# A batched trace of matrix products on one Trainium2 core: loads issued in strict order, smaller last loads with five rows for TensorE, and a first tile cut into five loads

**Chip, cores, metric.** One core of one Trainium2 chip. The metric is the device time of one execution in microseconds (us); medians of several executions are given.

## The reference

```python
def setup_inputs():
    B, N = 8, 2176
    return {"a": np.random.randn(B, N, N).astype(np.float32),
            "b": np.random.randn(B, N, N).astype(np.float32)}

def reference(a, b):
    prod = np.matmul(a, b)
    traces = np.diagonal(prod, axis1=1, axis2=2).sum(axis=-1)
    return traces.astype(np.float32)
```

The trace of A·B is the sum of the elementwise product of A transposed and B. So there is no matrix product to make: both inputs (303 MB in f32) are read once, A is transposed, and products are summed.

## The kernel before

A row in this text is a block of 128 matrix rows by 2176 columns; a batch has 17 of them (0 to 16). Only where the first tile is cut up, and in shares per DMA engine, a row is one matrix row (8704 bytes in f32). GpSimd issues the loads, which turn f32 to bf16 on the way. TensorE transposes A, ScalarE and VectorE copy the result out of PSUM, and VectorE multiplies it with B and sums, one row an instruction. In the last batch some rows are given to TensorE instead (a chain of 128x128 products into one PSUM tile, whose diagonal is the wanted sum): seven whole rows (every odd one up to 13) and parts of 14, 15 and 16. The last row comes in three pieces.

```python
    stage = ctx.enter_context(tc.tile_pool(name="stage", bufs=3))
    single = ctx.enter_context(tc.tile_pool(name="single", bufs=2))
    ...
    def load(src, start, m, count):
        if m == 1:
            t = single.tile([P, 1, N], bf16, tag="single")
        else:
            t = stage.tile([P, DOUBLE * ROWS, N], bf16, tag="stage")
        ...
        issued = nc.gpsimd.dma_start(out=part, in_=rows)
    ...
    def load_first(src, start):          # one row of A, in f32, by SyncE
        ...
        nc.sync.dma_start(out=plain, in_=src[start:start + P, :])
        nc.scalar.copy(out=t[:, 0, :half], in_=plain[:, :half])
        nc.vector.tensor_copy(out=t[:, 0, half:], in_=plain[:, half:])
    ...
        for start, m, count in joined(b_groups):      # joined: two groups of 4 in one load
            if last and start == N - P:
                b_t = stage.tile([P, DOUBLE * ROWS, N], bf16, tag="stage")
                row = b_t[:, 0, :]
                for g0, g1 in LAST_PIECES:            # [(0, 2), (2, 3), (3, 5)]
                    lo, hi = g0 * WIDE, min(g1 * WIDE, N)
                    nc.gpsimd.dma_start(out=row[:, lo:hi], in_=b[bi, start:start + P, lo:hi])
                ...
            for start, m, b_t in groups:
                for s in range(m):
                    if last and (m == 1 or s % 2 == 1):
                        half = 2 if m == 1 else 0
                        multiply_on_pe(at, row, v0 + s, half, len(a_groups))
                        if half:
                            on_dve(wide_at(at, v0 + s, 0, half), wide(row, 0, half))
                    else:
                        on_dve(wide_at(at, v0 + s, 0, n_wide), wide(row, 0, n_wide))
```

The framework decides from these when a load may be issued: the tile pools hand out buffers, and a load waits until the last reader of its buffer is done.

## Time and profile before

| | before |
|---|---|
| time, us (median; 711.01 to 711.58) | 711.17 |
| span of the profiled run, us | 709.4 |
| 16 DMA engines | 90% or more busy in 39 of 40 slices |
| VectorE / TensorE / ScalarE busy | 58% / 29% / 28% |
| rows 12-13 landed; row 14; row 15; third piece of row 16 | 699.75; 694.59; 702.42; 705.07 |
| pieces of row 16 issued | 691.92 |

The landings are worked out from the trace's completion signals: a load sends 16, one from each DMA engine, and is taken as landed with the last. The lines that carry the reading are in the prediction below. The view of the three pieces' tile says how early they were issued: the columns of its first line are least, median and longest duration in ns, then first and last start in us.

```profile
L247 POOL DMA_DIRECT2D b_t<-in_b_dram x3: 528/536/548, 691.9 to 693.0; - x3
DMA to landing us min/median/max: 11.7/11.8/12.1
```

Some 12 us pass from issue to landing, since the queue ahead of them is full. Such a wait costs nothing: a load that waits behind others keeps the engines fed.

### The profile page before, as it was taken

What the parts mean: (1) busy time and instruction counts of PE and PEld (TensorE: products, weight loads), DVE (VectorE), ACT (ScalarE), POOL (GpSimd) and SP (SyncE); (2) the same over time, 40 slices, a digit from 0 to 9 for tenths busy, and PEclk for the clock granted to TensorE, in tenths of its full rate; (3) what the DMA queues carried; (4) which work ended last, traced back from release to release, by engine and by line L of the source; (5) the groups of instructions that cost most, each with busy time, mean ns of one, the idle gap of its engine ahead of it and who ended that gap; (6) DMA issues with size and microseconds to landing.
All of it is one profiled execution on the core that took longest, in us unless ns stands there. A gap on an engine that the chain in (4) does not pass through costs nothing.

```text
span 709.4 us, 3709 instructions
## 1 busy us (share of the span) xinstructions
PE 206.3 (29%) x1406; PEld 193.0 (27%) x1406; DVE 411.4 (58%) x449; ACT 196.8 (28%) x210; POOL 34.6 (5%) x60
## 2 busy tenths in 40 slices
PE   1542005420065100542006510065100560005655
PEld 0542005410065100541005510065000550005655
DVE  0223996139952399514994259932599335993356
ACT  2443005430064200633006420065200651006610
POOL 1000000000010000100000000000000000000000
PEclk9977557765577655766557665577655775557776
DMA  9999999999999999999999999999999999999996
GB/s 220 220 220 219 206 219 220 219 217 209 219 220 218 217 212 216 220 219 215 212 218 220 218 213 215 215 222 217 215 214 213 225 217 212 215 217 222 219 207 138
DMA packets 11620, 152.32 MB, mean 215 GB/s; under 512 B 850, under 2 KB 1106, under 8 KB 3282
## 3 DMA queue, kind: packets, MB, share of 16 engines
q0 software_dynamic: 11456, 150.97, 100.1%
q1 hardware_dynamic: 146, 1.11, 0.4%
q8 instruction: 11, 0.18, 0.1%
q14 instruction: 7, 0.06, 0.0%
HBM read 303.04 MB, written 0.00 MB: 427 GB/s over the span
## 4 chain that ended last, share of the span: by engine, by line
DMA 56%; DVE 34%; issue 7%; PE 2%; another core or an unknown queue 2%; POOL 0%; DVEq 0%; POOLq 0%
DMA t<-in_b_dram 43%; DVE scratch L122 33%; DMA t<-in_a_dram 13%; PE ps L155 1%; DVE acc L122 0%; DVEq L122 0%; PE ps L176 0%; POOL identity masks.py:199 0%; DVE at L110 0%; POOL identity masks.py:197 0%; PE total L298 0%; DVE result L302 0%; DVE late L122 0%; POOLq L74 0%
## 5 line engine op out<-in xcount | busy, mean ns | idle before, releaser
L122 DVE CUSTOM_DVE_ANT_1 scratch<-at,t 128x2048 bf16<-128x2048 bf16 (+1 forms) x156 | 310.6, 1991 | 74.9 <-DMA t<-in_b_dram 67.7
L112 ACT COPY at<-ps 128x1024 bf16<-128x1024 bf16 x208 | 194.4, 1044 | 474.9 <-PE ps L155 474.5
L155 PE MATMUL ps<-identity,t 128*128 128x128 f32 x1071 | 177.9, 334 | 482.5 <-DVE sums L275 262.7
L155 PEld LDWEIGHTS ps<-identity,t 128*128 128x128 f32 x1071 | 166.2, 213 | 490.8 <-DVE sums L275 311.2
L110 DVE COPY at<-ps 128x1024 bf16<-128x1024 bf16 (+2 forms) x104 | 93.5, 902 | 214.4 <-PE ps L155 196.9
L74 POOL DMA_DIRECT2D t<-in_a_dram x23 | 15.3, 663 | 354.3 <-PE ps L176 156.5
L74 POOL DMA_DIRECT2D t<-in_b_dram x26 | 16.8, 645 | 288.3 <-PE ps L176 147.5
L283 PEld LDWEIGHTS <-at 128*128 128x128 bf16 x153 | 17.1, 122 | 13.3 <-issue 12.7
L283 PE MATMUL trace_ps<-t,at 128*128 128x128 bf16 x144 | 16.7, 293 | 12.3 <-DMA t<-in_b_dram 12.3
L176 PE MATMUL ps<-identity,t 128*128 128x128 bf16 x170 | 16.4, 219 | 4.9 <-DVE at L110 4.8
L176 PEld LDWEIGHTS <-t 128*128 128x128 bf16 x170 | 13.0, 100 | 8.3 <-issue 8.0
L122 DVE DVE_READ_ACCUMULATOR2_ANT acc<- 128x1 f32 x163 | 13.3, 81 | 0.0
L86 DVE CAST t<-words 128x1088 bf16<-128x1088 f32 x1 | 0.7, 726 | 4.8 <-DMA words<-in_a_dram 4.8
L247 POOL DMA_DIRECT2D b_t<-in_b_dram x3 | 1.6, 537 | 16.0 <-DVE acc L122 16.0
L122 DVE CUSTOM_DVE_ANT_0 scratch<-at,t 128x128 bf16<-128x128 bf16 x7 | 2.0, 291 | 0.2
L85 ACT CAST t<-words 128x1088 bf16<-128x1088 f32 x1 | 1.1, 1099 | 3.7 <-DMA words<-in_a_dram 3.7
L122 DVE CUSTOM_DVE_ANT_1 scratch<-at,b_t 128x256 bf16<-128x256 bf16 (+1 forms) x3 | 1.5, 510 | 0.1
L275 DVE TENSOR_REDUCE sums<-acc 128x1 f32<-128x22 f32 (+1 forms) x8 | 1.4, 174 | 0.3
L85 ACT ACT_TABLE_LOAD x1 | 1.3, 1283 | 0.7 <-PEq L321 0.7
L283 PE MATMUL trace_ps<-b_t,at 128*128 128x128 bf16 x9 | 1.3, 284 | 0.4 <-DMA b_t<-in_b_dram 0.4
L298 PE MATMUL total<-late,ones 128*1 128x1 f32 x8 | 0.8, 164 | 0.8 <-DVE late L122 0.8
L298 PEld LDWEIGHTS total<-late,ones 128*1 128x1 f32 x8 | 0.3, 80 | 1.2 <-DVE late L122 1.2
(14 smaller groups left out, 2.7 us busy)
## 6 DMA issues: line engine op xcount, KB each, us to landing
t<-in_a_dram POOLq DMA_DIRECT2D x16, 4352.0 KB, 46.7
t<-in_b_dram POOLq DMA_DIRECT2D x15, 4352.0 KB, 51.5
t<-in_b_dram POOLq DMA_DIRECT2D x9, 544.0 KB, 54.5
t<-in_a_dram POOLq DMA_DIRECT2D x7, 544.0 KB, 53.0
t<-in_b_dram POOLq DMA_DIRECT2D x1, 2176.0 KB, 42.9
words<-in_a_dram SPq DMA_DIRECT2D x1, 1088.0 KB, 4.9
t<-in_b_dram POOLq DMA_DIRECT2D x1, 1088.0 KB, 25.7
b_t<-in_b_dram POOLq DMA_DIRECT2D x1, 256.0 KB, 11.7
```

Source lines behind the costliest of these rows:

```text
L74: issued = nc.gpsimd.dma_start(out=part, in_=rows)
L85: nc.scalar.copy(out=t[:, 0, :half], in_=plain[:, :half])
L86: nc.vector.tensor_copy(out=t[:, 0, half:], in_=plain[:, half:])
L110: last_copy = nc.vector.tensor_copy(out=dst, in_=src)
L112: nc.scalar.copy(out=dst, in_=src)
L122: nc.vector.tensor_tensor_reduce(out=out, in0=x, in1=y, scale=1.0, scalar=0.0, op0=MUL, op1=ADD, accum_out=acc,)
L155: nc.tensor.transpose(ps[:, n * m + r, :], words[:, r, c0:c0 + step * (P - 1) + 1:step], tiles[f32],)
L176: last_transpose = nc.tensor.transpose(ps16[:, n, r, :], a_t[:, r, c0:c0 + P], tiles[bf16],)
L247: nc.gpsimd.dma_start(out=row[:, lo:hi], in_=b[bi, start:start + P, lo:hi])
L275: nc.vector.reduce_sum(out=tiles["sums"][:, bi:bi + 1], in_=acc[:, :cols], axis=mybir.AxisListType.X)
L283: nc.tensor.matmul(trace_ps, x, y, start=(n == 0), stop=(n == len(pe_work) - 1),)
L298: nc.tensor.matmul(total[:, BATCH - 1:BATCH], tiles["ones"], part, start=(n == 0), stop=(n == len(parts) - 1),)
```

## The change

Its intent: feed the DMA queue in program order, shorten what is left to do when the last bytes come (smaller last loads; TensorE gets rows 11, 12, 13 and 15 whole and most of 16, VectorE the others), and share the first tile differently over the 16 DMA engines. The diff, without its imports and empty lists (cuts marked with ...):

```diff
+    PE_ROWS = (11, 12, 13, 15)
+    FIRST_SPLIT = [(32, P, 1), (0, 32, 4), (1, 32, 4), (2, 32, 4), (3, 32, 4)]
...
+    def in_order():
+        return tc.issue_after(loaded[-1].ins) if loaded else nullcontext()
...
-        issued = nc.gpsimd.dma_start(out=part, in_=rows)
+        with in_order():
+            issued = nc.gpsimd.dma_start(out=part, in_=rows)
+        loaded.append(issued)
...
-        nc.sync.dma_start(out=plain, in_=src[start:start + P, :])
+        for lo, hi, step in FIRST_SPLIT:
+            nc.sync.dma_start(
+                out=plain[lo:hi:step, :], in_=src[start + lo:start + hi:step, :]
+            )
...
-        for start, m, count in joined(b_groups):
+        for start, m, count in ([(*g, 1) for g in b_groups] if last else joined(b_groups)):
...                                        (the pieces of the last row: in order, too)
-                    if last and (m == 1 or s % 2 == 1):
-                        half = 2 if m == 1 else 0
-                        multiply_on_pe(at, row, v0 + s, half, len(a_groups))
-                        if half:
-                            on_dve(wide_at(at, v0 + s, 0, half), wide(row, 0, half))
+                    if last and v0 + s in PE_ROWS:
+                        multiply_on_pe(at, row, v0 + s, 0, len(a_groups))
```

More of the change, by code (lines that the diff above doesn't have):

```diff
@@ L1 @@
 import math
-from contextlib import ExitStack
+from contextlib import ExitStack, nullcontext
 import concourse.bass as bass
@@ L64, in joined @@
         return loads
+    loaded = []
+    def in_order():
+        return tc.issue_after(loaded[-1].ins) if loaded else nullcontext()
     def load(src, start, m, count):
@@ L246 @@
                     lo, hi = g0 * WIDE, min(g1 * WIDE, N)
-                    nc.gpsimd.dma_start(out=row[:, lo:hi], in_=b[bi, start:start + P, lo:hi])
+                    with in_order():
+                        loaded.append(nc.gpsimd.dma_start(
+                            out=row[:, lo:hi], in_=b[bi, start:start + P, lo:hi]
+                        ))
                 multiply_on_pe(at, row, v0, 0, 1)
```

## The prediction

> **What bounds the kernel now.** I first read the forty slices and the queue table of the page, to see whether any compute engine matters at all.
>
> ```profile
> DVE  0223996139952399514994259932599335993356
> DMA  9999999999999999999999999999999999999996
> GB/s 220 220 220 219 206 219 220 219 217 209 219 220 218 217 212 216 220 219 215 212 218 220 218 213 215 215 222 217 215 214 213 225 217 212 215 217 222 219 207 138
> q0 software_dynamic: 11456, 150.97, 100.1%
> ```
>
> The 16 DMA engines are at 90% or more in all slices but the last, at a steady 205 to 225 GB/s; VectorE has long empty stretches in every batch. Loads from GpSimd take 100.1% of 16 engines' span for 150.97 MB (bf16 as landed). So the time is a head (until the engines run), the bytes at a fixed rate, and a tail (after the last bytes). The change leaves the bytes alone, so it can move only head, tail, and holes in the DMA queue. That is decided in the last 50 us, for which I read the timeline.
>
> ```profile
> 0.74 0.40 SPq L84 DMA_DIRECT2D words<-in_a_dram  x1
> 5.70 1.10 ACT L85 CAST t<-words 128x1088 bf16<-128x1088 f32 x1 [3.68 <-DMA words<-in_a_dram]
> ...
> 661.27 5.73 PE L155 MATMUL ps<-identity,t 128*128 128x128 f32 x28 [12.47 <-DMA t<-in_a_dram]
> 675.10 0.36 DVE L110 COPY at<-ps 128x384 bf16<-128x384 bf16 x1 [0.88 <-PE ps L176]
> 681.80 8.21 PE L283 MATMUL trace_ps<-t,at 128*128 128x128 bf16 x72 [6.74 <-DMA t<-in_b_dram]
> 691.92 1.59 POOL L247 DMA_DIRECT2D b_t<-in_b_dram  x3 [16.03 <-DVE acc L122]
> 692.07 4.22 PE L283 MATMUL trace_ps<-t,at 128*128 128x128 bf16 x36 [2.05 <-DMA t<-in_b_dram]
> 699.91 2.29 DVE L122 CUSTOM_DVE_ANT_1 scratch<-at,t 128x2048 bf16<-128x2048 bf16 x1 [3.09 <-DMA t<-in_b_dram]
> 702.24 1.23 DVE L122 CUSTOM_DVE_ANT_1 scratch<-at,t 128x1024 bf16<-128x1024 bf16 x1
> 703.51 1.22 DVE L122 CUSTOM_DVE_ANT_1 scratch<-at,t 128x1024 bf16<-128x1024 bf16 x1
> 704.86 0.68 DVE L122 CUSTOM_DVE_ANT_1 scratch<-at,b_t 128x512 bf16<-128x512 bf16 x1
> 705.11 0.45 PE L283 MATMUL trace_ps<-b_t,at 128*128 128x128 bf16 x3 [0.41 <-DMA b_t<-in_b_dram]
> 706.05 0.42 DVE L122 CUSTOM_DVE_ANT_1 scratch<-at,b_t 128x256 bf16<-128x256 bf16 x1
> 706.67 0.29 DVE L122 CUSTOM_DVE_ANT_0 scratch<-identity,trace_ps 128x128 bf16<-128x128 f32 x1 [0.18 <-DVE late L122]
> 707.42 0.32 SPq L303 DMA_DIRECT2D out_dram<-result  x1
> ```
>
> Three things stand here. The last bytes (the third piece of the last row) reach TensorE at 705.11. VectorE is unbroken from 699.91 to 706.96, so it, not the landing, sets the end by about a microsecond. And the three pieces of the last row were issued at 691.92, some 12 us before they landed: the queue never ran dry.
>
> One more fact comes from the trace's completion signals, 16 for each load, one a DMA engine. At the first whole load the 16 come within 0.45 us. The spread grows whenever a fetch on the two instruction queues (18 packets, 16 KB and 8 KB) falls on an engine: 1.58 at 68 us, 2.64 at the end. The third piece's signals run from 702.42 to 705.07, at lags of 0 to 0.57 us (six engines), 1.20 to 1.54 (seven) and 2.27 to 2.64 (three). The mean is 1.18, so perfect balance would land it 1.46 us earlier.
>
> **What the Trainium skill says.** "DMA: Bandwidth & Descriptors", section "Why a DMA increments its semaphore by 16 and not by 1": a DMA is spread over the largest count up to 16 that divides its slowest dimensions, on a SyncE queue over the lowest-numbered engines. A load of 96 rows then takes 6 rows on each of 16; a load of 8 rows takes engines 0 to 7. The trace agrees for 128 rows (16 signals; the split of 8 rows isn't in it). Its section "Latency and other measured facts" puts the first byte of a GpSimd DMA at about 1 us; no load here met an empty queue, so the trace can't confirm it. "Runtime: NRT & Kernel Launch", "Instruction fetch mechanics": instructions are refilled in blocks of 16 KiB by each sequencer's own DMA queue; the trace agrees with its 11 packets of 16384 bytes on the instruction queue, some 0.9 to 1.0 us each.
>
> **The change part by part.** *Strict order.* The built programs show that from the third batch on the single A tile was issued before the second A double; now it comes after. Neither position drains the queue (the last A double was issued at 614.16 and landed at 661, so over 20 us of work lay ahead of it). Worth to DMA: 0. The last double lands one row earlier: a row of 128x2176 f32 is 1.11 MB, at 434 GB/s read (twice the 217 GB/s that land as bf16 from 10 to 661 us) 2.57 us. Its transposes start at 658.5 and VectorE is free for B at 672.6 instead of 675.5.
>
> *Groups of 4, 4, 4, 2, 1, 1.* Landings, counted back at 2.57 us a row from row 15's 702.4 with the bytes unmoved: rows 0-3 at 671.4, 4-7 at 681.7, 8-11 at 692.0, 12-13 at 697.2, 14 at 699.75, 15 at 702.4.
>
> *Rows 11, 12, 13, 15 and most of 16 for TensorE.* VectorE now has 12 full rows (0 to 10 and 14) against 7 full and 2 halves; at some 2.37 us a row, 28.4 us against 19. It isn't on the path until the end: rows 0-3 from 672.6 to 682.1, 4-7 to 691.6, 8-10 from 692.1 to 699.2, row 14 from 699.85 to 702.2. It then waits for the pieces, where before it was busy until 704.8. With landings unmoved that takes 0.94 us off the end: the last small product starts at 705.15 in place of 706.05 (and the sum trims the rest). TensorE loses 64 matmuls, none of them last.
>
> *Where the gain goes.* In the built program the pieces' tile is put into the buffer of rows 12-13, and their issue waits for the last matmul of these two rows (before: the buffer of the first B load, free at 691.9). Those are 34 matmuls at 0.117 us (36 took 4.22), so 4.0 us after 697.2: 701.2. With 0.53 us for an issue and near 0.9 to the first byte (estimate, from the skill's 1 us) pieces flow from 702.6. The engines finish row 15 between 699.7 and 702.4, so all stand empty, 1.7 us on the mean. The pieces' 24 packets on each engine take 8 x (0.173 + 0.098 + 0.116) = 3.1 us, the signal 0.3: the last landing is 706.0, 0.9 later than before. That eats the 0.94.
>
> From the last landing to the end: 0.7 us to the start of the trace product, and 709.4 - 706.67 = 2.73 after it, 3.43 in all. 706.0 + 3.43 = 709.4: the old span.
>
> *First tile split.* 96 rows over 16 engines (6 each) and four loads of 8 rows over eight engines (4 more on each) make 10 rows on eight and 6 on the others, against 8. A row's packet takes 0.328 us, so 0.66 us are shifted, and stay shifted since the queue never drains. If the eight that get less are those that fetches hold up, every last signal moves by -0.66: rows 12-13 land at 696.5 and all that hangs on them comes 0.66 earlier. If it is the wrong side, +0.66. The split only makes sense if its author saw the former, but nothing in this trace names the engine of a packet: I give it two in three. Its own cost at the head (five issues of 0.4 us, the cast perhaps some us later) is hidden, since the next load that needs that buffer has until 46 us.
>
> Sum: 0 (bytes) - 0.94 (VectorE tail) + 0.9 (late pieces) and -0.66 or +0.66. Measured times lie 1.75 above the profiled span: 710.5 if the split helps, 711.2 if it does nothing, 711.9 if it hurts.
>
> **Rivals.** *The pieces come in time* (the 34 matmuls go faster, or first bytes need less than I think): then -0.94 - 0.66 = 709.6. Against it: 36 matmuls took 4.22 us in both late groups. *The bubble is worse* (first byte after 2 us, or TensorE reaches these rows late): 711.5 to 712. For it: GpSimd's issue is not measured on an empty queue here. *VectorE becomes the bound*: 12 rows are 28.4 us and it has from 672.6 to 702.4, with a slack of some 1.4 us; if copies of A end 3 us later than I count, row 14 ends at 703.5 and still before the last piece. Worth at most +0.5. *Strict order opens a hole* when an earlier load's buffer is late: would show as a slice under 200 GB/s and cost several us; buffers come free 20 us ahead, so one in thirty. *All is hidden*: a head and tail of some 10 us in 711 can't give 2% (14 us) either way.
>
> **Range and chances.** The three cases of the split, weighed, give 710.8. The uncertain terms are first byte and bubble (0.5 us each way), split (0.66), execution noise (0.2). Eight in ten: 709.6 to 712.0. A 2% change needs 14.2 us: no mechanism above has it.
>
> **What would show it.** The pieces' issue near 701 with TensorE's product as releaser (not 692); VectorE idle before its 128x512 product; the last landing at 705.3 to 706.6; a spread of the last signals near 2 us if the split is right, near 3.3 if wrong; 64 matmuls fewer. Wrong would be: an issue near 692, a middle slice that sags, or an end over 3.5 us after the last landing.

## The result, and the profile after

713.32 us (713.26 to 713.57) against 711.17: 2.15 us slower, outside the range of 709.6 to 712.0. The ratio is 1.003, with a 95% interval of 1.0013 to 1.0047. (Ratios here are the mean time of one kernel's fast runs over that of the other's of the same rounds, so not quite the ratio of the medians.)

The slices and the queue table of the changed kernel:

```profile
GB/s 211 219 218 218 209 224 212 218 219 213 221 218 214 215 219 219 218 213 217 213 219 218 218 214 218 215 217 216 218 216 218 212 218 216 218 218 211 219 214 116
q0 software_dynamic: 11472, 150.97, 99.8%
q1 hardware_dynamic: 178, 1.11, 0.6%
```

The middle is unmoved (217 GB/s from 10 to 700 us in both kernels); the slices that differ by more than the scatter are the first (211, was 220) and the last (116, was 138). So strict order made no hole, and the loss lies in head and tail. The chain of waits that ended last, in its final stretch (start, duration, what):

```profile
683.73 14.87 DMA t<-in_b_dram
698.64 4.08 PE trace_ps L299 x34
703.00 1.04 POOL b_t L264 x2
704.04 4.28 DMA b_t<-in_b_dram
708.37 0.50 PE trace_ps L299 x3
```

Before, this stretch was landings and VectorE alone. Now it goes from a landing (rows 12-13) to 34 products on TensorE, to GpSimd's issue, to the pieces' landing: the step foretold under "where the gain goes". The timeline has the same events with the releaser of each:

```profile
0.74 3.22 SPq L98 DMA_DIRECT2D words<-in_a_dram  x5
16.48 0.73 DVE L102 CAST t<-words 128x1088 bf16<-128x1088 f32 x1 [15.61 <-DMA words<-in_a_dram]
...
673.53 0.36 DVE L126 COPY at<-ps 128x384 bf16<-128x384 bf16 x1 [0.87 <-PE ps L192]
698.64 4.17 PE L299 MATMUL trace_ps<-t,at 128*128 128x128 bf16 x35 [2.75 <-DMA t<-in_b_dram]
703.00 1.60 POOL L264 DMA_DIRECT2D b_t<-in_b_dram  x3 [17.68 <-PE trace_ps L299]
703.89 2.12 PE L299 MATMUL trace_ps<-t,at 128*128 128x128 bf16 x17 [1.08 <-DMA t<-in_b_dram]
706.73 0.69 DVE L138 CUSTOM_DVE_ANT_1 scratch<-at,b_t 128x512 bf16<-128x512 bf16 x1 [2.86 <-DMA b_t<-in_b_dram]
708.45 0.43 DVE L138 CUSTOM_DVE_ANT_1 scratch<-at,b_t 128x256 bf16<-128x256 bf16 x1 [0.54 <-DMA b_t<-in_b_dram]
709.07 0.29 DVE L138 CUSTOM_DVE_ANT_0 scratch<-identity,trace_ps 128x128 bf16<-128x128 f32 x1 [0.18 <-PE total L314]
```

Set these beside the lines of before: VectorE now stands idle for 2.86 us until the first piece comes, where it was working without a break. GpSimd was held 17.68 us, and its releaser is TensorE. Row 15, which was the last thing in the queue, has landed by 703.85, but the pieces' first bytes come at 704.24: all 16 engines stood empty. The view of the pieces' tile confirms it from its own side, with a landing only some 4 us after the issue:

```profile
L264 POOL DMA_DIRECT2D b_t<-in_b_dram x3: 533/548/558, 703.0 to 704.0; - x3
DMA to landing us min/median/max: 3.7/3.8/4.3
```

A short time from issue to landing is bad news here: nothing was queued ahead.

The completion signals show the second loss. This table is worked out from the trace of each kernel; "mean" is the mean of the 16 signals of row 15's load, "excess" the last minus the mean.

| kernel | row 15 first | mean | last | excess | third piece |
|---|---|---|---|---|---|
| before | 699.71 | 700.89 | 702.42 | 1.53 | 705.07 |
| changed | 699.86 | 701.65 | 703.85 | 2.20 | 708.33 |
| e1, no split | 699.95 | 701.18 | 702.62 | 1.44 | 706.95 |
| e2, own buffer | 699.76 | 701.52 | 703.74 | 2.22 | 706.41 |
| e3, both | 700.04 | 701.26 | 702.84 | 1.58 | 705.55 |
| e4, split alone | 699.92 | 701.61 | 703.66 | 2.05 | 706.36 |
| e5, e3 with an even split | 700.65 | 701.99 | 703.57 | 1.58 | 706.31 |
| e7, e3 with a strided split | 700.40 | 701.66 | 702.97 | 1.31 | 705.62 |
| e8, e3 with double skew | 699.39 | 701.64 | 704.53 | 2.89 | 707.24 |
| e9, strict order alone | 700.02 | 701.26 | 702.73 | 1.47 | 705.28 |
| e11, e3 again | 699.99 | 701.02 | 702.53 | 1.51 | 705.25 |
| e12, e9 again | 699.87 | 701.06 | 702.82 | 1.76 | 705.15 |

The last two rows show the noise of one profile: the same kernel's mean moved by 0.2 us, its excess by up to 0.3.

### The profile page after: what moved, and what is told of

The parts are those of the page before. It is cut to its first block, busy times and chain, and to the rows that moved or that the text cites. A ratio compares the mean times of both kernels' runs of the same rounds, so it can differ in the third digit from the quotient of the medians.

```text
span 711.8 us, 3598 instructions
## 1 busy us (share of the span) xinstructions
PE 195.4 (27%) x1342; PEld 181.4 (25%) x1342; DVE 420.5 (59%) x455; ACT 196.5 (28%) x210; POOL 35.0 (5%) x61
## 4 chain that ended last, share of the span: by engine, by line
DMA 57%; DVE 35%; issue 5%; PE 2%; SPq 0%; ACT 0%; POOL 0%; another core or an unknown queue 0%; DVEq 0%; POOLq 0%; ACTq 0%
DMA t<-in_b_dram 48%; DVE scratch L138 34%; DMA t<-in_a_dram 6%; DMA words<-in_a_dram 2%; PE ps L171 1%; PE trace_ps L299 1%; DMA b_t<-in_b_dram 1%; DVE at L126 1%; DVE acc L138 0%; SPq L98 0%; ACT L101 0%; ACT t L101 0%; POOL b_t L264 0%; PE ps L192 0%
## 5 line engine op out<-in xcount | busy, mean ns | idle before, releaser
L138 DVE CUSTOM_DVE_ANT_1 scratch<-at,t 128x2048 bf16<-128x2048 bf16 (+1 forms) x159 | 319.6, 2010 | 76.4 <-DMA t<-in_b_dram 68.9
L171 PE MATMUL ps<-identity,t 128*128 128x128 f32 x1071 | 173.9, 328 | 484.3 <-DMA t<-in_a_dram 301.3
L171 PEld LDWEIGHTS ps<-identity,t 128*128 128x128 f32 x1071 | 162.1, 213 | 493.2 <-DVE sums L291 376.9
L299 PEld LDWEIGHTS <-at 128*128 128x128 bf16 x89 | 9.8, 124 | 25.4 <-issue 24.7
L299 PE MATMUL trace_ps<-t,at 128*128 128x128 bf16 x80 | 9.7, 291 | 22.8 <-DMA t<-in_b_dram 22.3
```

The lines of the kernel that those rows point to most:

```text
L138: nc.vector.tensor_tensor_reduce(out=out, in0=x, in1=y, scale=1.0, scalar=0.0, op0=MUL, op1=ADD, accum_out=acc,)
L171: nc.tensor.transpose(ps[:, n * m + r, :], words[:, r, c0:c0 + step * (P - 1) + 1:step], tiles[f32],)
L299: nc.tensor.matmul(trace_ps, x, y, start=(n == 0), stop=(n == len(pe_work) - 1),)
```

## The experiments

Each run was taken in the same rounds and on the same chip as the kernel before, whose median there is given in brackets. The runs e1 to e4 shared their rounds; so did e5 to e9 (no e6), and e10 to e12. The changed kernel was measured in another call (before: 711.17), so differences inside a group are the safer ones.

Theory A: the change has three effects. Strict order gains; the split loses; and the pieces' wait for TensorE's rows loses. Rivals: B, the split is harmless; C, order or smaller groups make holes in the queue; D, VectorE with 12 rows is the bound.

**e1: no split.**

```diff
-    FIRST_SPLIT = [(32, P, 1), (0, 32, 4), (1, 32, 4), (2, 32, 4), (3, 32, 4)]
+    FIRST_SPLIT = [(0, P, 1)]
```

> The changed kernel with its first tile loaded by one transfer of 128 rows again. Theory A (the split costs 1.4 us: rows 12-13 landed at 698.60 in place of 697.17, and it moves every last signal; the pieces' wait is a separate loss): rows 12-13 land near 697.2, the pieces' issue comes at 701.6 and not 703.0, the third piece lands near 706.9, spread of the 16 signals of row 15's load 2.6 us (4.0 in the changed kernel), time 712.0 +- 0.3. Rival B (the split is harmless, the whole loss is the pieces' wait for TensorE): 713.3. Rival C (strict order or the smaller B groups make holes in the queue): 713.3 too, with middle slices lower than before.

Measured: 712.16 (before, same rounds: 711.42), rows 12-13 landed at 697.37, the issue came at 701.77, the third piece at 706.95. As theory A had it; B and C are out. The split costs 1.2 us by the medians (713.32 - 712.16), 1.4 if each is taken against the kernel before in its own rounds.

**e2: a buffer of its own for the last row.**

```diff
+    tail = ctx.enter_context(tc.tile_pool(name="tail", bufs=1))
-                b_t = stage.tile([P, DOUBLE * ROWS, N], bf16, tag="stage")
+                b_t = tail.tile([P, 1, N], bf16, tag="tail")
```

> The changed kernel with the last row's tile in a buffer of its own, so that its three pieces wait for no other buffer; the split stays. Theory A: pieces issued near 685, right behind row 15; no empty queue; they land 2.65 us behind row 15's 703.9, at 706.5 in place of 708.3; span 709.9, time 711.7 +- 0.3. Rival B (the pieces' wait is the whole loss): landing at 705.1 and time near 710.2. Rival D (VectorE's 12 rows are the bound, the pieces only seem late): time stays at 713.

Measured: 711.67 (before 711.42). From its timeline, the issue of the pieces and VectorE's last products on them:

```profile
685.15 1.62 POOL L265 DMA_DIRECT2D b_t<-in_b_dram  x3
705.00 0.69 DVE L139 CUSTOM_DVE_ANT_1 scratch<-at,b_t 128x512 bf16<-128x512 bf16 x1 [1.25 <-DMA b_t<-in_b_dram]
706.54 0.43 DVE L139 CUSTOM_DVE_ANT_1 scratch<-at,b_t 128x256 bf16<-128x256 bf16 x1 [0.36 <-DMA b_t<-in_b_dram]
```

The last product starts at 706.54, not 708.45. The pieces' wait costs 1.65 us by the medians (713.32 - 711.67), 1.9 by the landings (708.33 against 706.41) and 1.8 inside one group of rounds (e1 - e3, 712.16 - 710.38). D is out: VectorE works the same 12 rows and waits for landings. The rows are not the matter but which buffer the pieces are put in.

**e3: both edits.**

> Both undone: first tile in one transfer, last row's tile in its own buffer; strict order, groups of 4, 4, 4, 2, 1, 1 and the five TensorE rows stay. Theory A: last landing 705.1 as in the kernel before, then 3.45 us to the end, where the kernel before needs 4.33: span 708.5, time 710.3 +- 0.3, 0.9 faster than before. Rival C (order or groups cost something): 711 or more. Rival D (VectorE bound by 12 rows): 711 or more, VectorE without idle time ahead of its 128x512 product.

Measured: 710.38 (710.16 to 710.77; before 711.42, 710.98 to 711.56), ratio 0.9986 (0.9974 to 0.9999). The executions do not overlap. It beats both kernels, the changed one by some 3 us. Against e2, in the same rounds, it puts the split at 1.3 us (711.67 - 710.38).

**e4: the split alone, in the kernel before.**

```diff
-        nc.sync.dma_start(out=plain, in_=src[start:start + P, :])
+        for lo, hi, step in FIRST_SPLIT:  (as in the change)
```

> The kernel before with the split of the first tile alone. Theory A: all last signals 1.4 us later (third piece at 706.5, spread of row 15's signals near 4.0 where it was 2.7); the kernel before has 0.95 us of VectorE work behind its last landing that hides part of it, so time 711.2 + 0.5 to 1.4, near 711.9. Rival B (split harmless): 711.2.

Measured: 712.58 (before 711.42), ratio 1.0017. The split costs 1.2 us here as well (712.58 - 711.42, same rounds); no part of it is hidden, against what I expected. In its timeline VectorE's last stretch starts with rows 12-13, which land late too (701.05), so the whole stretch moves:

```profile
701.20 2.29 DVE L127 CUSTOM_DVE_ANT_1 scratch<-at,t 128x2048 bf16<-128x2048 bf16 x1 [3.12 <-DMA t<-in_b_dram]
```

**e5: an even split, on e3.**

```diff
-    FIRST_SPLIT = [(0, P, 1)]
+    FIRST_SPLIT = [(32, P, 1), (0, 32, 1)]
```

> The kernel of e3 (own buffer, 710.4) with the first tile as a load of rows 32-127 and a load of rows 0-31, both over all 16 engines (6 + 2 rows each): the slow start of the split without its uneven share. In the split kernels the packets of the 96-row load took up to 0.6 us, not 0.33, and by 10 us 200 to 330 KB less had been read, 0.5 to 0.75 us at 434 GB/s. Theory A1 (the split costs by its slow start and by its uneven share, about half each): the start stays slow, spread of the last signals falls back to some 2.8, time 711.0 +- 0.3. A2 (all is the uneven share): 710.4. A3 (all is the slow start): 711.7 as with the whole split.

Measured: 711.44 (before 711.14), 0.3 above before, where e3 was 1.0 (and its repetition e11 0.7) below its own. The stretch of the first 10 us of the kernel before, of the changed one and of e5 (us; busy time and instructions of the engines; granted clock, DMA share, GB/s):

```profile
0.00:10.00 10.00, 2.06 (x9) 1.72 (x9) 1.01 (x3) 4.30 (x4) 3.31 (x11) 1.00 0.84 223
```
```profile
0.00:10.00 10.00, 0.00 (x0) 0.00 (x0) 0.06 (x1) 0.00 (x0) 2.59 (x10) 1.00 0.88 205
```
```profile
0.00:10.00 10.00, 0.00 (x0) 0.00 (x0) 0.79 (x2) 1.73 (x2) 2.60 (x10) 1.00 0.87 202
```

The engines are no less busy (0.84 to 0.88) but move less: 223, 205, 202 GB/s. This rate counts bytes as they land, so it depends on the mix of f32 (first tile) and bf16; the bytes read by 10 us, worked out from the packets, are free of that: 3236, 2905 and 2752 KB. So there is a slow start even with an even share: e5's mean moves 0.73 us later than e3's (0.97 than e11's), its excess stays at 1.58. The measured time lies outside the expected 711.0 +- 0.3: e5's slow start is dearer than the one it was to isolate. A1 holds in kind; that its two halves are equal isn't shown.

**e7: a strided split, on e3.**

```diff
-    FIRST_SPLIT = [(0, P, 1)]
+    FIRST_SPLIT = [(n, P, 4) for n in range(4)]
```

> The kernel of e3 with the first tile as four loads of 32 rows, every fourth row, each over 16 engines (2 rows each): four issues, even share, every load spread evenly over the partitions. If the slow packets come from the 96-row load's lying on 96 of the 128 partitions: packets of 0.33 us again, bytes by 10 us as in e3 (3170 KB), time 710.4 to 710.6. If they come from cutting the load at all (more issues): slow as in e5, 711.0.

Measured: 710.86 (before 711.14). Neither answer: it lies between. Packets of the first tile take 428 ns on the mean, against 390 in e3 and 550 in e5, and by 10 us 2927 KB had been read (e3 3170, e5 2752). So cutting the load costs something even with four equal parts, and e5's two parts cost more. That this comes from the load on 96 partitions isn't shown: in e5 the last 32 packets to start (as many as its load of rows 0-31 has) took 600 ns on the mean, the 96 before them 533. What slows them stays open.

**e8: double skew, on e3.**

```diff
-    FIRST_SPLIT = [(0, P, 1)]
+    FIRST_SPLIT = [(64, P, 1)] + [(n, 64, 8) for n in range(8)]
```

> The kernel of e3 with 64 rows over 16 engines and eight loads of 8 rows: 12 rows on eight engines and 4 on the others, twice the uneven share of the change (10 and 6). Theory A1: against e3, spread of the last signals grows by some 2.5 us (e2 with the single share: +1.2), last landing by some 1.3 to 2, time 712.4 +- 0.5. A3 (only the slow start counts): as with the single share, 711.7, if the start loses no more than there.

Measured: 712.85 (712.20 to 713.96; before 711.14), third piece at 707.24. The excess rises in step with the skew: 1.58 (8 rows on each engine), 2.22 (10 and 6), 2.89 (12 and 4), that is 0.64 and 0.67 for two rows more, near the 0.66 of the prediction's arithmetic. The spread (first to last signal) is 5.14, 2.35 more than e3's 2.79 (2.5 was expected). The start is no slower than with the single share (2949 KB read by 10 us, e2 2962), yet every execution is above A3's 711.7. A3 is out.

**e9: strict order alone, in the kernel before.** (Only `in_order` from the change.)

> The kernel before with strict order of issue alone (no split, groups and TensorE rows as before). Rows 12-13 then land ahead of row 14, at 697.2 and not 699.75, so VectorE does row 12 before row 14 comes and isn't late at the end. Theory A: the 0.95 us of VectorE work behind the last landing goes by the order alone, pieces issued near 692 as before: span 708.5, time 710.3 +- 0.3, the same as e3. Rival E (the gain of e3 comes from the five TensorE rows): stays 711.3.

Measured: 710.48 (710.28 to 710.71; before 711.14, 710.93 to 711.50), ratio 0.999 (0.9978 to 1.0003). The interval just includes 1; that the gain is real rests on executions that do not overlap, here and in e12, and on the trace: from the third piece's landing to the end are 3.4 us (705.28 to 708.7), where the kernel before needs 4.3 (705.07 to 709.4). Its timeline:

```profile
697.52 2.29 DVE L129 CUSTOM_DVE_ANT_1 scratch<-at,t 128x2048 bf16<-128x2048 bf16 x1 [0.49 <-DMA t<-in_b_dram]
700.10 1.23 DVE L129 CUSTOM_DVE_ANT_1 scratch<-at,t 128x1024 bf16<-128x1024 bf16 x1 [0.28 <-DMA t<-in_b_dram]
702.86 1.23 DVE L129 CUSTOM_DVE_ANT_1 scratch<-at,t 128x1024 bf16<-128x1024 bf16 x1 [1.53 <-DMA t<-in_b_dram]
705.41 0.43 DVE L129 CUSTOM_DVE_ANT_1 scratch<-at,b_t 128x256 bf16<-128x256 bf16 x1
```

VectorE meets each row as it lands and idles between (before it had them all at once from 699.91). The order alone removes the VectorE work that was left over behind the last landing; rival E is out.

**e10: smaller groups and TensorE rows alone** (the changed kernel with `in_order` doing nothing and no split).

> Groups of 4, 4, 4, 2, 1, 1 and the five TensorE rows alone: no strict order, no split. The built program then issues rows 12-13 last before the pieces, and the pieces still wait for TensorE's 34 products of these rows. Theory A (that wait is a cost of the groups and the row choice, and strict order only softens it): rows 12-13 land at 702.5, TensorE ends with them at 706.6, pieces issued at 706.7, first bytes 1.2 us later, last landing 4.1 us after that at 712.0, end 3.45 later: time 717.2 +- 0.8. Rival F (strict order is what makes the pieces wait): 711 or less.

Measured: 717.35 (before 711.21), ratio 1.0086. Its timeline:

```profile
702.44 5.99 PE L299 MATMUL trace_ps<-t,at 128*128 128x128 bf16 x52 [5.39 <-DMA t<-in_b_dram]
706.76 1.59 POOL L264 DMA_DIRECT2D b_t<-in_b_dram  x3 [21.41 <-PE trace_ps L299]
710.56 0.69 DVE L138 CUSTOM_DVE_ANT_1 scratch<-at,b_t 128x512 bf16<-128x512 bf16 x1 [6.22 <-DMA b_t<-in_b_dram]
```

Every event lies within 0.2 us of its forecast. Without strict order rows 12-13 come last before the pieces, and the kernel stands 6.1 us above the one before; strict order puts rows 14 and 15 between, which fill most of the hole. F is out: the order softens this wait.

**e11 and e12: e3 and e9 again, side by side.**

> e3 once more, beside e9 on one chip, to see whether groups and TensorE rows bring anything over strict order alone. Theory A (both remove the same 0.95 us of VectorE work behind the last landing): within 0.2 of e9, near 710.4. Rival: e3 ahead by 0.4 or more, since its VectorE waits 1.2 us before its last products and e9's does not.

> e9 once more, beside e3: 710.4, and 0.7 to 1.0 below the kernel before.

Measured: 710.47 (710.32 to 710.65) and 710.64 (710.49 to 710.80), before 711.21. Both are ahead of the kernel before (711.13 to 711.95) by 0.6 to 0.7 and equal within 0.2; their executions overlap. So smaller groups and TensorE rows bring nothing to speak of over the order alone, once their wait is taken away.

## Why the prediction was wrong, point by point

*What bounds it, and that bytes and middle don't move:* right (slices above).

*The pieces' wait ("Where the gain goes"):* right in kind, found in the built program; two of its three terms were too small. From the landing of rows 12-13 to the issue 4.4 us (698.60 to 703.00: the 34 products 4.08, then 0.28 to the issue), put at 4.0; from issue to first byte 1.24 (703.00 to 704.24), put at 1.4; from first byte to the last landing 4.09 (to 708.33), put at 3.4. The first packets on the empty engines took up to 1.06 us where later ones of the same size took 0.173, the only figure that the prediction used. Together some 0.9 us, with the split out of it: e1 is at 712.16 where the prediction's sum without a split was 711.2.

*"First tile split ... I give it two in three":* the step that failed, twice. The uneven share added some 0.66 where -0.66 was held likelier: as the excess rises by just the added rows (e3, e2, e8), the engine that comes last is among the eight that got more. (The sign given for the wrong side, a spread near 3.3, moved the last signal alone; the first comes 0.66 earlier too, and row 15 shows 3.99.) And "its own cost at the head ... is hidden" was wrong: the casts, at 16.48 and 17.74 in place of 5.70, are hidden (e8's tile lands at 29.4 us, and its start is no slower). They come late because in the trace each packet of the last three 8-row loads, and each 4-byte signal behind it, comes after a 17408-byte packet of GpSimd's load (1.30 us): these loads landed at 10.54, 13.45 and 16.35. But the engines move less in the first 10 us, and as they never rest again this is not won back. The means of row 15 give 0.26 us for it in e2 against e3 (0.50 against e11) and 0.76 in the changed kernel against the kernel before; the whole split costs 1.2 to 1.3 in time (e4 against before, e2 against e3).

With the split on the wrong side alone the prediction had 711.9, inside its range. It took the 0.9 us of the pieces' wait and the slow start of some 0.3 to 0.8 on top to leave it.

*"Strict order ... Worth to DMA: 0":* right for DMA, and the free VectorE at 673.8 came 1.2 us after the 672.6 foretold, which cost nothing; but the place of its worth was wrong. The prediction credited the 0.94 us of VectorE's tail to the smaller groups and TensorE rows; e9 shows that the order alone brings it (0.6 to 0.7 us measured).

*From the last landing to the end:* 3.43 foretold, 711.78 - 708.33 = 3.45 measured.

*A reading that was too strong:* that the spread of the signals grows "whenever" a fetch falls on an engine. In the kernel before it stayed at 1.5 to 1.6 through nine fetches, from 68 to 440 us. It did step up after others (to 1.84, 2.36 and 2.64), but no run here removes a fetch, so that they cause it is argued and not shown.

The sum from the kernel before, as measured: order -0.66 (e9); smaller groups and TensorE rows with their wait +1.40 on top of it (e1 stands 0.74 above the kernel before of its rounds, e9 0.66 below); split +1.16 (e4 against before) to +1.29 (e2 against e3). That makes +1.9 to +2.0; the measured change is +2.15, and the kernel before itself has medians from 711.14 to 711.42. Open: what makes the packets of a first tile that is cut up slow.

## What to carry to other kernels

In a kernel bound by DMA, ask of the last loads what their issue waits for, in the built program: a tile pool may hand the last tile the buffer of one whose readers finish last, and a buffer of its own, 4 KB per partition, was worth 1.8 us. The order in which loads land can matter more than how work is shared: the order alone gave the whole gain here. And an uneven share over the DMA engines stayed to the end of a queue that never drained (e2, e8), so shift one only when it is known which engines are late.

## What the Trainium skill lacked or had wrong

- "Runtime: NRT & Kernel Launch", section "Instruction fetch mechanics", calls the cost of crossing a 16 KiB boundary "mostly hidden". Here a fetch of 16 KB took 0.9 to 1.0 us of a DMA engine that the loads needed; the spread of a load's 16 signals grew from 0.45 to 2.7 us over the kernel before, in steps that follow some of the fetches (the cause isn't shown). No page has the seven fetches of 8192 bytes (0.32 us each).
- "DMA: Bandwidth & Descriptors", section "Why a DMA increments its semaphore by 16 and not by 1", agrees in the count of engines (an 8-row load shows 9 signals, one at once and eight later). What the pages lack is what it costs to cut a load on an idle queue: "SBUF — State Buffer", section "Door 1: The DMA port swizzle", has measured rates for partition ranges that start at 0 alone. Here the packets of the first tile took 504 ns on the mean in the changed kernel and 550 in e5, against 390 in one load, and by 10 us 2905 and 2752 KB were read in place of 3236.
- "DMA: Bandwidth & Descriptors", section "Latency and other measured facts", puts the first byte of a GpSimd DMA near 1 us; on the empty queue it was 1.24 us from the start of the issue (1.23 in e1, 1.24 in e10), and the first packets of 2 KB took 0.2 to 1.06 us where later ones took 0.173. No page has the second.
